# The output gate of the linear attention as one token-major group of 1024 features, and the attention values' writes issued by ScalarE

## The chip, the cores and the metric

The kernel runs on one core of a Trainium2 chip. The metric is the device time of one execution in microseconds (us). Three executions of the kernel before took 965.9, 2431.07 and 965.85 us; the median, 965.9 us, is the figure to beat. A further execution was profiled, and every duration below comes from it.

## The reference, cut to what matters

One layer of a decoder, 512 tokens of 1024 features, fp32, batch 1:

```
h   = RMSNorm(x)
q | k | v | r | low-rank gate | 3 x (attention q, k, v) | gA | gB  =  h @ w_in
oA  = RMSNorm_per_head(gated linear attention(q, k, v)) * silu(r)      4 heads, 256 features each
oB  = dilated attention, 3 groups of 4 heads, group results weighted and added
x  += (sigmoid(gA) * (oA @ w_o_gla) + sigmoid(gB) * (oB @ w_o_attn)) @ w_out
x  += relu(RMSNorm(x) @ w_mlp1)^2 @ w_mlp2
x  += sigmoid(RMSNorm(x) @ w_pg) * (p @ w_pp)
out = RMSNorm(x)
```

The change touches `r`, the gate of the linear attention (1024 columns of w_in), its product with the attention's result oA, and the values v of the attention groups 1 and 2.

## The kernel before, in words

**Products.** An fp32 operand is kept as a pair hi + lo, each of which TensorE takes in one pass; a product is three matmuls, hi·hi, hi·lo and lo·hi. The weights come as 250 operands of 128 x 1024 (512 KB each). `fetch` (L267) walks through them in order: DVE makes lo of operand i (L276), ScalarE hi of operand i+1 (L281), the sums for i+2 are made (`sums`), and the loads for i+3 are issued (`prepare`). Most projections of 512 columns use Winograd's form of Strassen's scheme, with 7 products in place of 8: the operands A11, S1, A22, S2, A12, S4, S3, where S1 = A21 + A22 and S3 = A11 + A21 (up to sign) are sums made by accumulating DMAs that POOL issues into the buffer of the first term (L243 for S1, L258 for S3), and S2 and S4 are sums by DVE (L255, L261). L258 stands right behind L255 in `sums`: DVE's S2 reads A11, then the DMA adds A21 onto A11's buffer, and the seventh product, S3, needs the result.

**Two forms.** `strassen` keeps the weights stationary and streams 256 tokens: 168 matmuls of 256 columns for 512 features, with the result feature-major (a tile holds 128 features). `wide` keeps the activations stationary and streams 512 weight columns: 168 matmuls of 512 columns for 1024 features, with the result token-major (a tile holds 128 tokens x 512 features). In both, ScalarE copies partial sums out of PSUM when a bank has its first product (L369 in `strassen`), and DVE adds the later bank to that copy (`add`, L422).

**Order.** The order on each engine is that of the program text. Every piece of matmuls calls `step`, which takes one callback off the list `later` and lets the first two generators of the list `side` go on by one step per `pace[0]` streamed columns. So work of DVE, ScalarE and POOL, and small groups of matmuls, are laid between the large products by count, not by time. The large products follow each other as k0, q1, k1, q2, k2, v12, v0, gq, gk, gv, oa, r0, r1, gb0, gb1, ga0, ga1, og, wo, then the feed-forward part. v12 (a `wide`), v0, r0 and r1 (each a `strassen`) are those that the change bears on.

**Values.** `values_cls("v12")` makes the values of attention groups 1 and 2. As each of its 8 token-major results is ready, POOL writes it to a DRAM scratch (L767); when a group's fourth is written, POOL reads the four residue classes back by stride (L772). POOL's queue holds, in program order, these writes and reads, the accumulating DMAs L243 and L258, and the exchange of the attention groups' weights: a write of a 16 x 128 tile (L879, `k_dram`) and its read back (L880, `cc`), which DVE's L896 needs.

**Gate.** `gates("r", ...)` runs `strassen` twice (r0, r1). Behind each addition ScalarE applies Sigmoid (L1197) and DVE multiplies (L1201), giving silu(r) as 8 feature-major tiles `rg[j]`. The linear attention runs head by head as generators `gla(h)`: transposes of k by TensorE (L1026), small scores (L1032, L1035), the lo half of the transposed k by DVE (L1039), and products with the values (L976). `gla_out(h)` transposes the head's token-major result (L1126), and DVE multiplies it out of PSUM by the norm's weight and by `rg[j]` (L1129). `gla_split`, started in ga0, makes the pairs `og[j]` (ScalarE L429, DVE L437), which the product og needs.

Of the kernel before, what the change touches and what calls it, by code (L numbers as in the profile page):

```python
# [13 lines left out]
AF = mybir.ActivationFunctionType  # L14
OP = mybir.AluOpType
# [4 lines left out]
P = 128  # L20
T = 512
D = 1024
KC = D // P
# [23 lines left out]
def weight_units():  # L47

    u = []

    def fm(name, src, col, n, row=0):
        for j in range(n):
            u.append((f"{name}.{j}", "fm", src, row, col + j * P))

    def tm(name, src, col):
        for i in range(4):
            u.append((f"{name}.{i}", "tm", src, i * 2 * P, col))

    def quad(name, src, col, kind="quad", chunk=0):
        for m, k in ((0, 0), (1, 0), (1, 1), (0, 1)):  # L60
            u.append((f"{name}.A{m + 1}{k + 1}", kind, src, 2 * chunk + k, col + m * (P if kind == "quad" else 256)))

    def quadw(name, src, cs):

        for m, k in ((0, 0), (1, 0), (1, 1), (0, 1)):
            for i in range(2):
                u.append((f"{name}.A{m + 1}{k + 1}.{i}", "quadw", src, 2 * i + k, cs[m]))

    fm("k0", "w_in", att_col(0, 1), 4)
    fm("q1", "w_in", att_col(1, 0), 4)  # L70
    quad("k1", "w_in", att_col(1, 1))
    quad("q2", "w_in", att_col(2, 0))
    quad("k2", "w_in", att_col(2, 1))
    quadw("v12", "w_in", (att_col(1, 2), att_col(2, 2)))
    quad("v0", "w_in", att_col(0, 2), "quadt")
    quad("gq", "w_in", GQ)
    quad("gk", "w_in", GK)
    quadw("gv", "w_in", (GV, GV + 512))
    for j in range(4):
        u.append((f"oa.{j}", "half", "w_o_attn", 0, j * 2 * P))  # L80
    quad("r0", "w_in", GR)
    quad("r1", "w_in", GR + 512)
    for i in range(2):
        quad(f"gb{i}", "w_in", GATE + D + i * 512)
    for i in range(2):
        quad(f"ga{i}", "w_in", GATE + i * 512)
    fm("og", "w_o_gla", 0, 8)
    fm("wo", "w_out", 0, 8)
    for q in range(8):
        quad(f"m1q{q}", "w_mlp1", q * 512)  # L90
    for what, sub, c in MLP2:
        if what == "plain":
            for kk in range(4 * c, 4 * c + 4):
                u.append((f"m2s{sub}.{kk}", "tm", "w_mlp2", kk * 2 * P, sub * 512))
        else:
            quad(f"m2s{sub}c{c}", "w_mlp2", sub * 512, chunk=c)
    for j in range(2):
        u.append((f"pp{j}.0", "tm", "w_pp", 0, j * 512))
    for j in range(2):
        tm(f"pg{j}", "w_pg", j * 512)  # L100
    return u
# [80 lines left out]
def block_kernel(ctx, tc, xT, ws, pT, wts, wha, wa2, vec, lnf, rel, onehot, ident_d, mask_d, out):  # L182
# [13 lines left out]
    def u32(name="u"):  # L196
        return ar.tile([P, T], F32, tag="u", name=name)
# [11 lines left out]
    side, later = [], []  # L209
# [125 lines left out]
    def halves(t):  # L335
        return slice(t * HT, (t + 1) * HT)
# [47 lines left out]
    def wide(name, xo, finish):  # L384


        bank, sums = {}, {}

        def begin(m, t, n, b):
            def go():  # L390
                sums[m, t, n] = u32()
                S.activation(sums[m, t, n], bank[b][n], AF.Copy, scale=-1.0 if m else 1.0)
            return go

        def end(m, t, n, b):
            return lambda: finish(m, t, n, sums.get((m, t, n)), bank[b][n])

        for i, (op, xname, b) in enumerate(WIDE):
            fresh = b not in bank
            if fresh:  # L400
                bank[b] = [smt() if b == "b" else mmt() for _ in range(2)]
            for pr in range(4):
                wh, wl = weight(f"{name}.{op}.{pr // 2}")
                xh, xl = xo(xname, pr)
                r = slice((pr % 2) * 512, (pr % 2 + 1) * 512)
                mms = []
                for n in range(2):
                    c = slice(n * P, (n + 1) * P)
                    for k, (l, w) in enumerate(((xh, wh), (xl, wh), (xh, wl))):
                        mms.append((bank[b][n], l[:, c], w[:, r], fresh and not pr and not k, pr == 3 and k == 2))  # L410
                run(mms, 3, shared=True)
            if i in WBEGIN:
                (m, t), b = WBEGIN[i]
                later[0:0] = [begin(m, t, n, b) for n in range(2)]
            if i in WEND:
                (m, t), b = WEND[i]
                later.extend(end(m, t, n, b) for n in range(2))
# [8 lines left out]
    def split_hi(x, col=None):  # L426
        hi = u32r()
        if col is None:
            S.activation(hi, x, AF.Copy)  # L429
        else:  # L430
            S.activation(hi, x, AF.Copy, scale=col)
        return hi

    def split_lo(x, hi, col=None):
        lo = u32r()
        if col is None:
            V.tensor_tensor(lo, x, hi.bitcast(F32), op=OP.subtract)  # L437
        else:
            V.scalar_tensor_tensor(out=lo, in0=x, scalar=col, in1=hi.bitcast(F32), op0=OP.mult, op1=OP.subtract)
        return hi, lo  # L440
# [5 lines left out]
    def split_later(x, res, j):  # L446

        def first():
            hi = split_hi(x)
            later.append(lambda: res.__setitem__(j, split_lo(x, hi)))  # L450
        later.append(first)
# [288 lines left out]
    def whole(m, s, ps):  # L740

        if s is None:
            s = u32()
            S.activation(s, ps, AF.Copy, scale=-1.0 if m else 1.0)
        else:
            add(m, s, s, ps)
        return s
# [12 lines left out]
    def values_cls(name):  # L760

        v_dram = [dr.tile([T, 512], F32, name=f"v{m}_dram") for m in range(2)]
        res, left = [[], []], [4, 4]

        def finish(m, t, n, s, ps):
            s, r = whole(m, s, ps), (2 * t + n) * P
            GP.dma_start(v_dram[m][r:r + P, :], s)  # L767
            left[m] -= 1
            if not left[m]:
                for c in range(4):  # L770
                    v = u32()
                    GP.dma_start(v, v_dram[m].rearrange("(m c) f -> c m f", c=4)[c])  # L772
                    res[m].append(v)

        wide(name, xs_op, finish)
        return res

    def softmax(ps, n0, bias, nm, sums, col, prob):
# [338 lines left out]
            yield  # L1117

    def gla_out(h):
        for f in range(2):  # L1120
            j = 2 * h + f
            while rg_done[j] < 2:
                yield
            pts = smt()
            for p in range(4):
                TE.transpose(pts[:, p * P:(p + 1) * P],  # L1126
                             ons_[h][p // 2][:, (p % 2) * 256 + f * P:(p % 2) * 256 + (f + 1) * P], ident)
            yield
            V.scalar_tensor_tensor(out=rg[j], in0=pts, scalar=cv[:, C_GN + j:C_GN + j + 1], in1=rg[j],  # L1129
                                   op0=OP.mult, op1=OP.mult)  # L1130

    def gla_split():
        for j in range(KC):
            split_later(rg[j], og, j)
            yield


    side.append(setup())
# [38 lines left out]
    for j in range(KC):  # L1177
        y = u32()
        S.activation(y, fm(None, oa, (j % 2) * 512, weight(f"oa.{j // 2}")), AF.Copy)
        S.dma_start(y_dram[j], y)  # L1180
    rg, tb, ga = [], [], []
    rg_done = [0] * KC

    def gates(name, i, res, make):

        new = [u32() for _ in range(4)]
        res.extend(new)

        def finish(m, t, s, ps):
            add(m, s, s, ps)  # L1190
            later.append(lambda: make([4 * i + 2 * n + m for n in range(2)], [new[2 * n + m][:, halves(t)] for n in range(2)], s, t))

        strassen(f"{name}{i}", xs_op, finish)

    def silu(js, outs, s, t):
        g = u32()
        S.activation(g, s, AF.Sigmoid)  # L1197

        def mult():
            for n in range(2):  # L1200
                V.tensor_tensor(outs[n], s[:, halves(n)], g[:, halves(n)], op=OP.mult)  # L1201
                rg_done[js[n]] += 1
        later.append(mult)

    def sigmoid(js, outs, s, t):
        for n in range(2):
# [3 lines left out]
        while later:  # L1210
            later.pop(0)()

    gates("r", 0, rg, silu)
    side.extend(gla_out(h) for h in range(2))
    gates("r", 1, rg, silu)
    pace[0] = 4096
    side.extend(gla_out(h) for h in range(2, 4))
    for i in range(2):
        gates("gb", i, tb, sigmoid)

# [9 lines left out]
    later.extend(merge(j) for j in range(KC))  # L1230
    for i in range(2):
        gates("ga", i, ga, sigmoid)
        if i == 0:
            side.append(gla_split())
    drain()
    pace[0] = 2048
    mix = [None] * KC
# [351 lines left out]
    def put(tt, c):  # L1589
        n = c.stop - c.start  # L1590
        o = u32()
        V.scalar_tensor_tensor(out=o[:, 0:n], in0=x2t[4 + tt][:, c], scalar=fr[:, tt:tt + 1], in1=lnb[1][:, c],
                               op0=OP.mult, op1=OP.mult)
        SY.dma_start(out[tt * P:(tt + 1) * P, 512 + c.start:512 + c.stop], o[:, 0:n])
# [112 lines left out]
```

## Time and profile before

| | us |
|---|---|
| median of 3 executions | 965.9 |
| the profiled execution | 968.71 |
| its span, first to last instruction | 966.9 |
| TensorE busy in the span | 954.6 (99%) |
| VectorE (DVE) busy | 740.6 (77%) |
| ScalarE (ACT) busy | 543.9 (56%) |
| POOL busy | 101.5 (10%) |
| mean granted TensorE clock | 0.994 |

PE is TensorE's matmuls, PEld its weight loads, ACTq and POOLq the queues that issue DMAs. In a row of the timeline stand the start, the duration, engine, line, operation, out<-in and, in brackets, how long the engine was idle before and what ended that. In a row of the windows stand the stretch, its length, the busy time of each engine with its number of instructions, the granted clock of TensorE, the share of the DMA engines and GB/s. Groups of instructions have, behind the bar, the total, the mean of one in ns, and the idle time of the engine ahead of them.

### The profile page before, as it was taken

What the parts mean: (1) busy time and instruction counts of PE and PEld (TensorE: products, weight loads), DVE (VectorE), ACT (ScalarE), POOL (GpSimd) and SP (SyncE); (2) the same over time, 40 slices, a digit from 0 to 9 for tenths busy, and PEclk for the clock granted to TensorE, in tenths of its full rate; (3) what the DMA queues carried; (4) which work ended last, traced back from release to release, by engine and by line L of the source; (5) the groups of instructions that cost most, each with busy time, mean ns of one, the idle gap of its engine ahead of it and who ended that gap; (6) DMA issues with size and microseconds to landing.
All of it is one profiled execution on the core that took longest, in us unless ns stands there. A gap on an engine that the chain in (4) does not pass through costs nothing.

```text
span 966.9 us, 16069 instructions
## 1 busy us (share of the span) xinstructions
PE 954.6 (99%) x6398; PEld 880.4 (91%) x6398; DVE 740.6 (77%) x1062; ACT 543.9 (56%) x886; POOL 101.5 (10%) x143
## 2 busy tenths in 40 slices
PE   9999999989999999999999999999999999999997
PEld 8789998889998899999988889999998998998886
DVE  7698879746789669988765788777767999787754
ACT  7357547435575569776632346555655664354633
POOL 0140010220100012023001000010000000000000
PEclk9999999989999999999999999999999999999999
DMA  9374373965636554546526437556564374553102
GB/s 325 116 233 119 117 175 72 300 197 132 147 94 199 170 154 117 146 132 196 153 88 196 131 71 182 162 134 173 155 173 109 110 176 107 134 194 109 44 0 88
DMA packets 42923, 140.97 MB, mean 146 GB/s; under 512 B 6435, under 2 KB 7023, under 8 KB 42848
## 3 DMA queue, kind: packets, MB, share of 16 engines
q1 hardware_dynamic: 28224, 95.37, 29.3%
q0 software_dynamic: 12096, 42.17, 21.5%
q10 hardware_dynamic: 2528, 2.41, 0.7%
q8 instruction: 50, 0.82, 0.3%
q14 instruction: 25, 0.20, 0.1%
HBM read 133.60 MB, written 8.17 MB: 147 GB/s over the span
## 4 chain that ended last, share of the span: by engine, by line
PE 92%; DVE 3%; ACT 2%; DMA 1%; issue 1%; POOL 0%; POOLq 0%; DVEq 0%; ACTq 0%
PE mmt L295 77%; PE smt L295 6%; PE mmt L552 2%; PE smt L976 1%; DMA w<-in_wts_dram 1%; DVE lo L276 1%; PE smt L916 1%; PE smt L839 1%; DVE u L422 0%; PE smt L524 0%; ACT hi L281 0%; PE smt L933 0%; PE smt L809 0%; PE smt L932 0%; PE smt L922 0%
## 5 line engine op out<-in xcount | busy, mean ns | idle before, releaser
L295 PE MATMUL mmt<-ur,hi 128*128 128x256 f32 (+1 forms) x3120 | 635.8, 301 | 0.0
L295 PEld LDWEIGHTS mmt<-ur,hi 128*128 128x128 f32 x3120 | 500.7, 188 | 21.8
L295 PE MATMUL mmt<-ur,lo 128*128 128x256 f32 (+1 forms) x1560 | 470.7, 302 | 0.0
L276 DVE TENSOR_TENSOR lo<-w,hi 128x1024 fp32r<-128x1024 f32 x250 | 303.2, 1219 | 57.3 <-PE mmt L295 27.7
L281 ACT ACTIVATE hi<-w 128x1024 fp32r<-128x1024 f32 x250 | 260.9, 1054 | 110.6 <-PE mmt L295 25.9
L295 PEld LDWEIGHTS mmt<-ur,lo 128*128 128x128 f32 x1560 | 294.0, 188 | 10.9
L295 PE MATMUL mmt<-hi,ur 128*128 128x512 f32 (+3 forms) x480 | 134.7, 366 | 4.3 <-ACT u L369 4.3
L429 ACT ACTIVATE ur<-u 128x512 fp32r<-128x512 f32 x130 | 77.2, 624 | 98.1 <-DVE u L1241 30.8
L295 PEld LDWEIGHTS mmt<-hi,ur 128*128 128x128 f32 x480 | 87.0, 193 | 17.0 <-ACT u L369 4.5
L422 DVE TENSOR_TENSOR u<-u,mmt 128x512 f32<-128x512 f32 (+1 forms) x116 | 73.1, 655 | 38.1 <-PE mmt L295 37.9
L437 DVE TENSOR_TENSOR ur<-u,ur 128x512 fp32r<-128x512 f32 x129 | 84.8, 686 | 16.5 <-ACT ur L429 16.1
L295 PE MATMUL mmt<-lo,ur 128*128 128x512 f32 (+3 forms) x240 | 87.2, 363 | 0.0
L369 ACT ACTIVATE u<-mmt 128x512 f32<-128x512 f32 x88 | 52.3, 594 | 52.8 <-PE mmt L295 52.4
L243 POOL DMA_DIRECT2D w<-in_wts_dram x32 | 28.8, 923 | 309.6 <-DMA w<-in_wts_dram 102.8
L258 POOL DMA_DIRECT2D w<-in_wts_dram x24 | 21.2, 884 | 332.6 <-DVE w L255 239.8
L295 PEld LDWEIGHTS mmt<-lo,ur 128*128 128x128 f32 x240 | 46.3, 193 | 6.6
L295 PE MATMUL smt<-ur,hi 128*128 128x512 f32 x160 | 50.4, 393 | 0.1
L295 PEld LDWEIGHTS smt<-ur,hi 128*128 128x128 f32 x160 | 29.7, 188 | 8.1 <-PE smt L649 0.8
L295 PE MATMUL smt<-ur,lo 128*128 128x512 f32 x80 | 31.2, 390 | 0.0
L255 DVE TENSOR_TENSOR w<-w 128x1024 f32<-128x1024 f32 x24 | 29.4, 1225 | 0.8
L261 DVE TENSOR_TENSOR w<-w 128x1024 f32<-128x1024 f32 x24 | 29.4, 1225 | 0.8
L462 ACT ACTIVATE u<-u 128x512 f32<-128x512 f32 x24 | 14.9, 622 | 16.7 <-DVE u L1322 16.7
(213 smaller groups left out, 767.8 us busy)
## 6 DMA issues: line engine op xcount, KB each, us to landing
w<-in_wts_dram SPq DMA_DIRECT2D x170, 512.0 KB, 4.4
w<-in_wts_dram POOLq DMA_DIRECT2D x56, 512.0 KB, 5.7
u<-in_xT_dram SPq DMA_DIRECT2D x8, 256.0 KB, 5.0
u<-in_ws_dram SPq DMA_DIRECT2D x8, 256.0 KB, 5.2
v_dram<-u POOLq DMA_DIRECT2D x8, 256.0 KB, 9.1
u<-v_dram POOLq DMA_DIRECT2D x8, 256.0 KB, 6.1
y_dram<-u ACTq DMA_DIRECT2D x8, 256.0 KB, 3.6
u<-y_dram POOLq DMA_DIRECT2D x8, 256.0 KB, 5.9
```

The source lines that it names most:

```text
L243: GP.dma_start(w, wts[UNIT[b]], accum_op=OP.add)
L255: V.tensor_tensor(w, w, raw[f"{q}.A11"], op=OP.add)
L258: GP.dma_start(w, wts[UNIT[f"{q}.A21"]], accum_op=OP.add)
L261: V.tensor_tensor(w, w, raw[f"{q}.A12"], op=OP.add)
L276: V.tensor_tensor(lo, w, hi.bitcast(F32), op=OP.subtract)
L281: S.activation(hi, w, AF.Copy)
L295: TE.matmul(o, lhsT=l, rhs=r, start=a, stop=b, skip_group_check=shared)
L369: S.activation(sums[c], bank[b], AF.Copy, scale=-scale if c[0] else scale)
L422: V.tensor_tensor(out, s, ps, op=OP.subtract if m else OP.add)
L429: S.activation(hi, x, AF.Copy)
L437: V.tensor_tensor(lo, x, hi.bitcast(F32), op=OP.subtract)
L552: TE.matmul(q0ps[i], lhsT=(hi, hi, lo)[j][:, c], rhs=(xh, xl, xh)[j], start=not k and not j, stop=k == KC - 1 and j == 2)
```

## The change

It has three parts.

1. The two `strassen` of the gate, r0 and r1, become one `wide("r")` on 1024 columns. Sigmoid and product are one ScalarE and one DVE instruction of 128 x 512 per result, and silu(r) is kept as 8 token-major tiles `rg[m, 2t + n]`.
2. `gla_out(h)` waits for the four gate tiles of its half, multiplies the head's token-major result by them in place (four DVE instructions of 128 x 256), then transposes, and the pair `og[j]` is made straight out of PSUM, the norm's weight as the scale. `gla_split` is gone. All four `gla_out` are put on the side list ahead of the gate's product, and the line that set the pace to 4096 from r1 on is gone, so it stays 3072 through gb0 to ga1.
3. In `values_cls` the 8 writes go onto ScalarE's queue, each as a callback behind the addition, and the 8 reads are issued by a generator that starts when all 8 writes are issued.

```diff
-    quad("r0", "w_in", GR)
-    quad("r1", "w_in", GR + 512)
+    quadw("r", "w_in", (GR, GR + 512))
...
         def finish(m, t, n, s, ps):
             s, r = whole(m, s, ps), (2 * t + n) * P
-            GP.dma_start(v_dram[m][r:r + P, :], s)
-            left[m] -= 1
-            if not left[m]:
+
+            def put():
+                S.dma_start(v_dram[m][r:r + P, :], s)
+                left[0] -= 1
+            later.append(put)
+
+        def back():
+            while left[0]:
+                yield
+            yield
+            for m in range(2):
                 for c in range(4):
                     v = u32()
                     GP.dma_start(v, v_dram[m].rearrange("(m c) f -> c m f", c=4)[c])
                     res[m].append(v)
+                yield
 
         wide(name, xs_op, finish)
+        side.append(back())
...
     def gla_out(h):
+        while not all((h // 2, p) in rg for p in range(4)):
+            yield
+        for p in range(4):
+            o = ons_[h][p // 2][:, halves(p % 2)]
+            V.tensor_tensor(o, o, rg[h // 2, p][:, halves(h % 2)], op=OP.mult)
+            if p % 2:
+                yield
         for f in range(2):
             j = 2 * h + f
-            while rg_done[j] < 2:
-                yield
             pts = smt()
...
             yield
-            V.scalar_tensor_tensor(out=rg[j], in0=pts, scalar=cv[:, C_GN + j:C_GN + j + 1], in1=rg[j],
-                                   op0=OP.mult, op1=OP.mult)
-
-    def gla_split():
-        for j in range(KC):
-            split_later(rg[j], og, j)
-            yield
+            c = cv[:, C_GN + j:C_GN + j + 1]
+            hi = split_hi(pts, c)
+            yield
+            og[j] = split_lo(pts, hi, c)
...
-    def silu(js, outs, s, t):
-        g = u32()
-        S.activation(g, s, AF.Sigmoid)
-
-        def mult():
-            for n in range(2):
-                V.tensor_tensor(outs[n], s[:, halves(n)], g[:, halves(n)], op=OP.mult)
-                rg_done[js[n]] += 1
-        later.append(mult)
+    def silu(m, t, n, s, ps):
+        s, g = whole(m, s, ps), u32()
+
+        def act():
+            S.activation(g, s, AF.Sigmoid)
+
+            def mult():
+                V.tensor_tensor(s, s, g, op=OP.mult)
+                rg[m, 2 * t + n] = s
+            later.append(mult)
+        later.append(act)
...
-    gates("r", 0, rg, silu)
-    side.extend(gla_out(h) for h in range(2))
-    gates("r", 1, rg, silu)
-    pace[0] = 4096
-    side.extend(gla_out(h) for h in range(2, 4))
+    side.extend(gla_out(h) for h in range(4))
+    wide("r", xs_op, silu)
...
         gates("ga", i, ga, sigmoid)
-        if i == 0:
-            side.append(gla_split())
```

POOL's queue around the end of v12 and through v0, before. L243 is an accumulation for S1, L258 for S3, L767 and L772 the writes and reads of the values, L879 and L880 the weights' exchange; the L258 in the middle is that of v0.

```order
L243 DMA w<-in_wts_dram 128x1024 x5
L767 DMA v_dram<-u 128x512 x4
L243 DMA w<-in_wts_dram 128x1024
L767 DMA v_dram<-u 128x512 x2
L772 DMA u<-v_dram 128x512 x4
L258 DMA w<-in_wts_dram 128x1024
L767 DMA v_dram<-u 128x512 x2
L772 DMA u<-v_dram 128x512 x4
L879 DMA k_dram<-u 16x128
L880 DMA cc<-k_dram 128x4x4
```

The same place in the changed kernel, where L243 is L242, L258 is L257, L772 is L779, and L879 and L880 are L888 and L889.

```order
L257 DMA w<-in_wts_dram 128x1024 x2
L242 DMA w<-in_wts_dram 128x1024 x6
L257 DMA w<-in_wts_dram 128x1024
L779 DMA u<-v_dram 128x512 x8
L888 DMA k_dram<-u 16x128
L889 DMA cc<-k_dram 128x4x4
```

The writes have left POOL's queue, v0's L257 stands ahead of all eight reads instead of behind the first four, and k_dram and cc still stand behind the last read.

ScalarE's queue at the same place in the changed kernel: L280 makes hi (L281 before), L768 are the writes, L743 and L368 copies out of PSUM.

```order
L280 ACTIVATE hi<-w 128x1024 x2
L768 DMA v_dram<-u 128x512 x2
L280 ACTIVATE hi<-w 128x1024 x2
L743 ACTIVATE u<-mmt 128x512 x2
L870 ACTIVATE e_1988<-e_1988 128x16
L871 ACTIVATE e_1989<-e_1989 128x16
L768 DMA v_dram<-u 128x512
L280 ACTIVATE hi<-w 128x1024
L368 ACTIVATE u<-mmt 128x512
L768 DMA v_dram<-u 128x512
L280 ACTIVATE hi<-w 128x1024
```

The rows shown are the last of three pairs of writes and the last two single ones; the seventh and eighth write stand at the start of v0's products, between hi operands.

TensorE around the linear attention's third head (h = 2), before: L1026 are its transposes of k (the second L1026 those of the fourth head), L976 its first products with the values, L295 the large products (here those of r1 and gb0).

```order
L1026 MATMUL smt<-ident,u 128x128 x3
...
L1032 MATMUL smt<-u 128x64 x4
L1035 MATMUL smt<-u 64x64 x4
...
L1026 MATMUL smt<-ident,u 128x128 x3
...
L295 MATMUL mmt<-ur,hi 128x256 x2
L976 MATMUL smt<-ur 128x256 x6
```

The same in the changed kernel (L1026 is L1035, L1032 and L1035 are L1041 and L1044, L976 is L985, L295 is L294; the large products are the end of `wide("r")` and then gb0).

```order
L1035 MATMUL smt<-ident,u 128x128 x3
L294 MATMUL mmt<-hi,ur 128x512 x2
...
L1041 MATMUL smt<-u 128x64 x4
L1044 MATMUL smt<-u 64x64 x4
...
L294 MATMUL mmt<-ur,hi 128x256
L985 MATMUL smt<-ur 128x256 x6
```

Before, 88 matmuls of 256 columns lie between the head's transposes and its first products with the values; after, 18 of 512 columns and 40 of 256, and the fourth head's transposes come later.

More of the change, by code (lines that the diff above doesn't have):

```diff
@@ L762, in values_cls @@
         v_dram = [dr.tile([T, 512], F32, name=f"v{m}_dram") for m in range(2)]
-        res, left = [[], []], [4, 4]
+        res, left = [[], []], [8]
         def finish(m, t, n, s, ps):
             s, r = whole(m, s, ps), (2 * t + n) * P
-            GP.dma_start(v_dram[m][r:r + P, :], s)
-            left[m] -= 1
-            if not left[m]:
+            def put():
[7 more added lines that the diff above has]
+            for m in range(2):
                 for c in range(4):
@@ L1180, in block_kernel @@
         S.dma_start(y_dram[j], y)
-    rg, tb, ga = [], [], []
-    rg_done = [0] * KC
+    rg, tb, ga = {}, [], []
     def gates(name, i, res, make):
```

## Prediction

> **What bounds the kernel now.** I read the profile's page first, then TensorE's waits, then the chain of waits, the timeline and the windows around the one long wait. The page:
>
> ```profile
> span 966.9 us, 16069 instructions
> PE 954.6 (99%) x6398; PEld 880.4 (91%) x6398; DVE 740.6 (77%) x1062; ACT 543.9 (56%) x886; POOL 101.5 (10%) x143
> ```
>
> TensorE is busy for 954.6 of 966.9 us. A gain can only be shorter matmul work or less of the 12 us of idling. Where TensorE waits for another engine:
>
> ```profile
> PE mmt L295 <- ACT u L369: 4.3, 1, 4.3
> PE smt L524 <- POOL ones L519: 1.0, 1, 1.0
> PE smt L976 <- DVE ur L1039: 0.2, 1, 0.2
> PE smt L916 <- ACT u L908: 0.2, 1, 0.2
> ```
>
> Columns: total us, times, longest. One wait of 4.3 us stands out. The chain of waits around it (start, us, what) and the timelines of POOL, DVE and TensorE:
>
> ```profile
> 194.34 0.44 POOL u L772
> ...
> 194.86 11.38 DMA w<-in_wts_dram
> ...
> 206.32 0.07 ACT hi L281
> ...
> 209.35 2.71 PE mmt L295 x11
> ```
>
> ```profile
> 192.75 2.13 POOL L772 DMA_DIRECT2D u<-v_dram  x4 [8.77 <-DMA v_dram<-u]
> 194.86 0.94 POOL L258 DMA_DIRECT2D w<-in_wts_dram  x1
> 195.42 1.48 POOL L767 DMA_DIRECT2D v_dram<-u  x2
> 208.43 2.14 POOL L772 DMA_DIRECT2D u<-v_dram  x4 [11.53 <-issue]
> 216.75 0.79 POOL L880 DMA_DIRECT2D cc<-k_dram  x1 [5.68 <-DMA k_dram<-u]
> ```
>
> ```profile
> 184.30 1.23 DVE L255 TENSOR_TENSOR w<-w 128x1024 f32<-128x1024 f32 x1
> ```
>
> ```profile
> 209.35 0.79 PE L295 MATMUL mmt<-hi,ur 128*128 128x256 f32 x2 [4.26 <-ACT u L369]
> ```
>
> The profile names ScalarE's copy L369, but the chain shows who was late. TensorE waits at v0's seventh product for hi of S3, which ScalarE starts only at 206.32, when the accumulation L258 has landed (11.38 us after its issue at 194.86). DVE's sum, behind which that DMA may go, ended at 185.53. It was issued 9.3 us later because POOL's queue had the first four value reads ahead of it, and POOL stood 8.77 us waiting for the value writes to land. Then the granted clock:
>
> ```profile
> core 0: us, PE busy (x) PEld busy (x) DVE busy (x) ACT busy (x) POOL busy (x), PEclk, DMA share, GB/s
> 187.60:204.80 17.20, 17.20 (x146) 17.14 (x145) 5.87 (x11) 4.11 (x8) 4.16 (x7) 1.00 0.78 240
> 204.80:209.40 4.60, 0.34 (x4) 0.13 (x2) 1.78 (x2) 3.08 (x5) 0.97 (x2) 0.91 0.13 46
> 209.40:215.30 5.90, 5.90 (x28) 5.90 (x29) 4.65 (x6) 3.44 (x4) 1.67 (x4) 0.50 0.82 265
> ```
>
> After the idle, 28 matmuls take 5.90 us at a clock of 0.50. The 146 of the first stretch took 17.20 us, 0.118 each, so 28 need 3.30. The clock costs 5.90 − 3.30 = 2.6 us, and the wait with its tail 4.26 + 2.6 = 6.9 us. The Trainium skill, "TensorE: Matmul & The Clock Gate", Part 1, has the clock drop to 4/8 after an idle window of about 3.4 µs and come back after a busy one; the row of 0.50 agrees, though the slow stretch here is longer than one such window.
>
> **The change part by part.**
>
> *Values' writes (part 3).* With the writes gone from POOL's queue and the reads behind L257, v0's accumulation goes when DVE's sum ends, at about 186. How long it takes to land:
>
> ```profile
> w<-in_wts_dram POOLq DMA_DIRECT2D x56, 512.0 KB, 5.7
> v_dram<-u POOLq DMA_DIRECT2D x8, 256.0 KB, 9.1
> ```
>
> Median 5.7 us, here 11.38: issued at 186.1 it lands at 192 to 197.5. From hi's start at 206.32 to TensorE's at 209.35 are 3.0 us, and TensorE is out of work at 209.35 − 4.26 = 205.1, so hi has to start by 202.1. Even at the longer landing 4.6 us are left. So the wait goes, and with it the half clock: **−6.9 us**. The bounds are 0 (a landing later by 4.6 us and the whole wait more) and −6.9, since TensorE has no other idle time there.
>
> What ScalarE takes over is 8 issues. POOL's own take
>
> ```profile
> L767 POOL DMA_DIRECT2D v_dram<-u x8 | 4.8, 648 | 4.9 <-DVE u L422 4.7
> 160.00:180.00 20.00, 20.00 (x90) 16.25 (x89) 16.16 (x19) 12.32 (x21) 3.08 (x5) 1.00 0.61 170
> 180.00:200.00 20.00, 20.00 (x139) 18.66 (x138) 12.10 (x20) 7.69 (x11) 6.17 (x10) 1.00 0.82 276
> ```
>
> 0.65 us each, 5.2 us in all, with up to 4.7 us of waiting for DVE's additions; ScalarE is idle for 20 of these 40 us. Behind a waiting issue stand hi operands, which are made an operand ahead; one of v12's 14 operands lasts TensorE 12 matmuls of 0.226 us (below), 2.7 us, so a write that waits a microsecond delays no product. I cost it at nothing; without this cover it would be at most the 5.2 us.
>
> What is late next: the reads of both groups. They wait for the last write, which stands behind v0's first copy on ScalarE, and DVE's consumer of cc stands behind k_dram and cc:
>
> ```profile
> 190.76 0.60 ACT L369 ACTIVATE u<-mmt 128x512 f32<-128x512 f32 x1 [1.31 <-PE mmt L295]
> 221.22 0.62 DVE L896 TENSOR_SCALAR u<-u,cc 128x256 f32<-128x256 f32 x2 [1.91 <-DMA cc<-k_dram]
> ```
>
> The last write goes at 191.4 instead of 196.9 and lands by 200.5 (9.1 later); the eight reads then take 2 x 2.13 us to issue, to 204.8, where before the last was issued at 210.6. k_dram needs 0.5 + 5.7 us (the wait in front of L880), cc about as much: it lands by 216.5 at the latest. It is needed 6.9 us earlier than before, at 212.4 to 214.3. So DVE waits 0 to 4 us where it waited 1.91, and TensorE went on meanwhile. I cost it at nothing; its upper bound is 2 us.
>
> *Gate as one wide group (part 1).* 336 matmuls of 256 columns become 168 of 512. Two stretches with almost only the one kind:
>
> ```profile
> 620.00:720.00 100.00, 100.00 (x845) 100.00 (x844) 73.62 (x85) 57.99 (x83) 7.72 (x9) 1.00 0.61 159
> 500.00:560.00 60.00, 60.00 (x266) 49.70 (x265) 38.11 (x56) 21.28 (x29) 6.12 (x10) 1.00 0.50 150
> ```
>
> 100 / 845 = 118.3 ns for 256 columns, with weight loads busy for all of it; 60 / 266 = 225.6 ns for 512, with the loads 83% busy. Thus 336 x 0.1183 = 39.75 against 168 x 0.2256 = 37.9: **−1.8 us**. Missing records would make both a little shorter: with 0.6 ns to either side the bounds are −1.5 and −2.1. The Trainium skill, "TensorE: Matmul & The Clock Gate", section "Back-to-back issue gap", gives N / 2.4 + 2.5 ns for a warm matmul, an estimate of 109 and 216 ns, by which 36.7 − 36.2 = −0.5 us; the rows are 9 and 10 ns above it and decide.
>
> The other engines' share:
>
> ```profile
> L422 DVE TENSOR_TENSOR u<-u,mmt 128x512 f32<-128x512 f32 x92 | 61.2, 684 | 33.1 <-PE mmt L295 32.9
> L437 DVE TENSOR_TENSOR ur<-u,ur 128x512 fp32r<-128x512 f32 x129 | 84.8, 686 | 16.5 <-ACT ur L429 16.1
> L1201 DVE TENSOR_TENSOR u<-u 128x256 f32<-128x256 f32 x16 | 6.0, 421 | 0.6 <-ACT u L1197 0.6
> L1129 DVE SCALAR_TENSOR_TENSOR u<-smt,cv,u 128x512 f32<-128x512 f32 x8 | 6.0, 745 | 0.0
> ```
>
> DVE: two additions fewer (two results have a single bank), −1.4; 16 products of 421 ns become 8 of about 684, −1.2; 16 new products of the token-major result at 421, +6.7; eight L1129 and eight L437 become eight lo straight from PSUM at 745, −5.5. Sum −1.4 us, so DVE's total hardly moves. ScalarE's hi now reads PSUM, its copies stay 8; SP loads A11's two operands a second time, as S3 overwrites them. The transposes of L1126 stay 32. None of this sets the end.
>
> *What moves in time.* The gate's stretch is where DVE and ScalarE have least room:
>
> ```profile
> 340.70:366.99 26.29, 26.29 (x226) 26.16 (x225) 17.40 (x27) 20.43 (x36) 2.26 (x3) 1.00 0.50 134
> 366.99:388.70 21.71, 21.71 (x185) 21.71 (x184) 19.43 (x36) 21.11 (x40) 5.72 (x5) 1.00 0.58 147
> 388.70:414.51 25.81, 25.60 (x221) 25.13 (x219) 24.48 (x42) 17.39 (x31) 2.25 (x3) 1.00 0.49 123
> ```
>
> These are r0, r1 and gb0. In gb0 DVE is busy for 24.48 of 25.81 us, and TensorE's only other wait falls there:
>
> ```profile
> 387.41 0.49 PE L1026 MATMUL smt<-ident,u 128*128 128x128 f32 x3
> ...
> 400.80 0.74 PE L976 MATMUL smt<-ur 128*128 128x256 f32 x4 [0.21 <-DVE ur L1039]
> ```
>
> Head 2's transposed k left TensorE at 387.41, its first products with the values were due 12.8 us later (400.19 or so, two of them went), and DVE's lo came 0.21 us late. Of these, 88 x 0.118 = 10.4 us were large matmuls and 2.4 transposes of two heads and scores. In the changed kernel 18 matmuls of 512 and 40 of 256 columns stand there, 18 x 0.226 + 40 x 0.118 = 8.8 us, and some 2.1 for one head's transposes and the scores: 10.9 us. So 1.9 us less, and DVE is the engine that is due: lo may be late by 1.9 + 0.2 = 2.1. Against that, the earlier half of the gate's work has room (17.40 of 26.29), and the order lists two table loads of ScalarE fewer, 1.28 us each:
>
> ```profile
> 390.13 1.28 ACT L1197 ACT_TABLE_LOAD   x1
> ```
>
> The bounds are 0 and +2.1; the slack of 2.3 us that DVE had in r1 (21.71 − 19.43) makes the lower one the nearer, so I take **+0.8 us**. An idle time of up to 2.1 us is shorter than the one that dropped the clock.
>
> **Sum.** −6.9 − 1.8 + 0.8 = −7.9 us. On the profiled execution: 968.71 − 7.9 = 960.8. That execution is 2.8 us above the median of 965.9, and the terms are the same on either, so 965.9 − 7.9 = **958.0 us**, −0.8%.
>
> **Rivals.**
>
> *The accumulation lands late all the same.* For it: the DMA engines are 78% busy over v0 and the landing took 11.38 us, twice the median. The writes now come sooner and more densely, ahead of it on the same engines. Against it: 4.6 us of room. If it keeps the wait, the change gives −1.8 + 0.8: **964.9 us**. The Trainium skill, "DMA: Bandwidth & Descriptors", section "Issuing engines are not separate DMA queues", says that issuing on several engines only saves the sequencer's time to issue; by that rule this is the result. The 8.77 us are POOL's waiting in queue order, not issue time, and no bandwidth is needed for them to go. 8 in 100.
>
> *DVE late at several heads.* Room in gb0 is 1.3 us, and the pace no longer goes to 4096, so the steps of heads 2 and 3 come a third closer together. If lo of k or of the gate's operands is late at three or four places by 1 to 1.5 us, 3 to 5 us go: 965.9 − 8.7 + 3 to 5 = **960 to 962**. Against it: −1.4 us of DVE work in all. 17 in 100.
>
> *Slower than before: one long wait in the gate's stretch with the half clock.* The wait for lo of head 2 grows past the 4.3 us that dropped the clock at 209. It then costs itself and 2.6 us. To outweigh −8.7 it has to be over 6.1 us: DVE's room of 2.3 and 1.3 us would have to turn into 6 us of arrears. At 7 us of wait: 965.9 − 8.7 + 9.6 = **966.8 us**. For it: DVE at 95% of gb0. Against it: DVE has 1.4 us less to do, and the tightening is 1.9 us. 4 in 100.
>
> *The stall goes, but matmuls of 512 do not gain here.* In r the small matmuls of the heads break the stream as well; then −6.9 + 0.8 and **959.8**. It lies within the likeliest case's range.
>
> **How the numbers follow.** The likeliest (71 in 100) is 958.0, its own range 956.5 to 960: from −1.8 − 6.9 with nothing late, 957.2, and with the matmul bound of −2.1, 956.9, to +2.1 late, 959.3. The rivals above reach 962 and 964.9. The range is **956 to 963**: the lower end allows 0.9 us for what I have not seen, the upper one takes in the second rival; out of it lie the first and the third rival with 12 in 100. A measurement of this kernel can tell about 2% (19.3 us) from no change. No case reaches that on the fast side, and on the slow side only something unforeseen: faster 0.01, same 0.97, slower 0.02.
>
> **What would show it right or wrong.** In the profile after, v0's L257 is issued before 188 and no PE wait of over 1 us stands in v0; the clock is 1.00 from 188 to 220. From the gate's first product to gb0's first are 46 us in place of 48.0. TensorE's waits name L1048 (lo of k) with 0 to 2.1 us. If v0's wait is still there, the queue was not its cause; if TensorE has a wait of over 3 us between 330 and 420, the second or third rival holds; if gb0's start is less than 1 us nearer to the gate's, the matmul term is wrong.

## The result, and the profile after

The changed kernel took 960.33 us (median of 6 executions, 959.87 to 960.66), the kernel before, on the same chip, 967.38 us; the ratio is 0.9928, 95% interval 0.9914 to 0.9943. One execution of the kernel before (2431.07 us) and one of the last kernel below (1576.4 us, granted clock 0.556) were slow by far and are left out of the ratios and ranges; without them the medians are 967.3 and 962.9 us. In three later jobs, on which the experiments rest, the kernel before had medians of 965.57, 965.09 and 964.47 us with single executions from 962.3 to 968.5, the changed kernel 959.91 us. So the level of the changed kernel is firm, and what scatters is the kernel before: in the last of these jobs the two stood 4.56 us apart, not 7.05.

The page of the changed kernel and TensorE's waits:

```profile
span 958.5 us, 15733 instructions
PE 950.3 (99%) x6230; PEld 869.3 (91%) x6230; DVE 739.4 (77%) x1060; ACT 542.0 (57%) x884; POOL 95.3 (10%) x135
```

```profile
PE smt L523 <- POOL ones L518: 1.0, 1, 1.0
PE smt L1140 <- DVE u L1133: 0.2, 1, 0.2
```

The wait of 4.3 us is gone, and of the waits inside the kernel one of 0.2 us is left, at a new place: the transposes L1140 wait for DVE's products with the gate, L1133. POOL's timeline, and the first hi behind the accumulation on ScalarE:

```profile
185.82 0.87 POOL L257 DMA_DIRECT2D w<-in_wts_dram  x1 [3.54 <-DVE w L254]
193.91 2.19 POOL L779 DMA_DIRECT2D u<-v_dram  x4 [7.22 <-PE mmt L294]
198.00 2.12 POOL L779 DMA_DIRECT2D u<-v_dram  x4 [1.90 <-issue]
208.13 0.80 POOL L889 DMA_DIRECT2D cc<-k_dram  x1 [7.50 <-DMA k_dram<-u]
```

```profile
195.66 1.06 ACT L280 ACTIVATE hi<-w 128x1024 fp32r<-128x1024 f32 x1 [1.67 <-DMA w<-in_wts_dram]
```

v0's accumulation goes when DVE's sum ends, 9 us earlier than before, and hi of S3 is made 10.7 us earlier. The reads still wait for the writes' landing, but nothing that TensorE needs soon stands behind them. The windows of v0's end, and of the gate's stretch as a whole (r to ga1), first after, then before:

```profile
204.80:209.40 4.60, 4.60 (x41) 4.60 (x41) 2.59 (x5) 2.12 (x2) 0.99 (x2) 1.00 0.10 35
209.40:215.30 5.90, 5.90 (x51) 5.71 (x50) 5.87 (x15) 1.67 (x4) 1.61 (x2) 1.00 0.78 158
...
333.04:474.45 141.41, 141.25 (x1041) 133.38 (x1039) 119.75 (x180) 104.60 (x199) 21.90 (x27) 1.00 0.58 156
```

```profile
340.70:483.22 142.52, 142.31 (x1209) 141.70 (x1208) 118.24 (x177) 106.51 (x201) 23.97 (x27) 1.00 0.55 151
```

No idle time and no half clock are left in v0. By stage, from each product's first matmul to the next one's, v0 went from 26.95 to 20.14 us, gq from 32.03 to 31.44 (the rest of the half clock and a wait of 0.2), and the gate's stretch from 142.52 to 141.41. That is −6.8, −0.6 and −1.1; with −0.25 at the start and about +0.4 behind ga1 the span fell by 8.4 us.

### The profile page after: what moved, and what is told of

The parts are those of the page before. It is cut to its first block, busy times and chain, and to the rows that moved or that the text cites. A ratio compares the mean times of both kernels' runs of the same rounds, so it can differ in the third digit from the quotient of the medians.

```text
span 958.5 us, 15733 instructions
## 1 busy us (share of the span) xinstructions
PE 950.3 (99%) x6230; PEld 869.3 (91%) x6230; DVE 739.4 (77%) x1060; ACT 542.0 (57%) x884; POOL 95.3 (10%) x135
## 4 chain that ended last, share of the span: by engine, by line
PE 96%; DVE 1%; issue 1%; ACT 1%; DMA 1%; POOL 0%; POOLq 0%; DVEq 0%; ACTq 0%
PE mmt L294 80%; PE smt L294 7%; PE mmt L551 2%; PE smt L985 1%; PE smt L925 1%; PE smt L848 1%; DMA u<-y_dram 1%; PE smt L523 0%; PE smt L818 0%; PE smt L942 0%; PE smt L941 0%; PE smt L931 0%; PE smt L817 0%; PE smt L1547 0%; PE smt L1041 0%
## 5 line engine op out<-in xcount | busy, mean ns | idle before, releaser
L294 PE MATMUL mmt<-ur,hi 128*128 128x256 f32 (+1 forms) x2896 | 594.8, 303 | 0.0
L294 PEld LDWEIGHTS mmt<-ur,hi 128*128 128x128 f32 x2896 | 465.9, 188 | 21.8
L294 PE MATMUL mmt<-ur,lo 128*128 128x256 f32 (+1 forms) x1448 | 438.9, 303 | 0.0
L280 ACT ACTIVATE hi<-w 128x1024 fp32r<-128x1024 f32 x250 | 261.1, 1054 | 105.3 <-PE mmt L294 30.0
L294 PEld LDWEIGHTS mmt<-ur,lo 128*128 128x128 f32 x1448 | 272.7, 188 | 10.9
L294 PE MATMUL mmt<-hi,ur 128*128 128x512 f32 (+3 forms) x576 | 162.5, 367 | 0.0
L428 ACT ACTIVATE ur<-u 128x512 fp32r<-128x512 f32 x122 | 72.3, 624 | 96.8 <-DVE u L1248 30.9
L294 PEld LDWEIGHTS mmt<-hi,ur 128*128 128x128 f32 x576 | 102.5, 188 | 15.9
L294 PE MATMUL mmt<-lo,ur 128*128 128x512 f32 (+3 forms) x288 | 105.0, 365 | 0.0
L436 DVE TENSOR_TENSOR ur<-u,ur 128x512 fp32r<-128x512 f32 x121 | 79.5, 685 | 16.6 <-ACT ur L428 16.2
L368 ACT ACTIVATE u<-mmt 128x512 f32<-128x512 f32 x80 | 47.4, 593 | 47.6 <-PE mmt L294 47.3
L242 POOL DMA_DIRECT2D w<-in_wts_dram x34 | 31.3, 959 | 335.1 <-DMA w<-in_wts_dram 139.0
L294 PEld LDWEIGHTS mmt<-lo,ur 128*128 128x128 f32 x288 | 54.2, 188 | 8.6
L257 POOL DMA_DIRECT2D w<-in_wts_dram x22 | 19.6, 889 | 319.2 <-DVE w L254 231.1
L294 PE MATMUL smt<-ur,hi 128*128 128x512 f32 x160 | 50.4, 393 | 0.1
L294 PEld LDWEIGHTS smt<-ur,hi 128*128 128x128 f32 x160 | 29.7, 188 | 8.1 <-PE smt L648 0.8
L294 PE MATMUL smt<-ur,lo 128*128 128x512 f32 x80 | 31.2, 390 | 0.0
```

What stands on the lines that cost most here:

```text
L242: GP.dma_start(w, wts[UNIT[b]], accum_op=OP.add)
L257: GP.dma_start(w, wts[UNIT[f"{q}.A21"]], accum_op=OP.add)
L280: S.activation(hi, w, AF.Copy)
L294: TE.matmul(o, lhsT=l, rhs=r, start=a, stop=b, skip_group_check=shared)
L368: S.activation(sums[c], bank[b], AF.Copy, scale=-scale if c[0] else scale)
```

## The experiments

**Part 3 alone.** The kernel before with the change's `values_cls` and nothing else of it.

> The kernel before with part 3 alone: the eight value writes on ScalarE's queue, the reads issued by the generator after the last write. The gate stays as before. My theory (POOL's queue order made v0's accumulation late; the half clock follows from the wait) expects v0 to take 20.1 us instead of 26.95, gq 31.4 instead of 32.0, no TensorE wait of over 1 us and the clock at 1.00 throughout: 7.4 us less in the trace, a ratio of 0.9924 (0.991 to 0.994). The rival, that most of the gain comes from the gate, expects 0.997 or more.

960.90 against 965.57 us, ratio 0.9949 (0.9931 to 0.9967). In its trace v0 takes 20.14 us and gq 31.42, and no wait of TensorE is over 1.0 us. So the trace behaves as forecast, but the gain between executions is 4.7 us and not 7.4, and the ratio lies outside the 0.991 to 0.994 that I expected. Part 3 is most of the change; my size for it is too large.

**Parts 1 and 2 alone.** The changed kernel with the old `values_cls`.

> The changed kernel with the values' writes and reads as before (POOL, in the old order), so parts 1 and 2 alone. My theory expects the wait of 4.3 us and the half clock in v0 to stand as before, and 1.1 us less over the gate's stretch (r to ga1, 142.5 us before): a ratio of 0.9989 (0.998 to 1.000). The rival, that the gate's change gains more than its matmuls show, expects below 0.997.

964.41 us, ratio 0.9991 (0.9977 to 1.0004). The stretch r to ga1 takes 141.63 us. TensorE's wait in v0 is there, smaller than in the first profile, and the clock falls all the same (its timeline, then two windows with the granted clock, third from the end):

```profile
207.21 0.51 PE L294 MATMUL mmt<-hi,ur 128*128 128x256 f32 x2 [2.42 <-ACT u L368]
```

```profile
204.51:207.92 3.41, 0.99 (x9) 0.78 (x8) 2.44 (x3) 3.41 (x5) 0.69 (x2) 1.00 0.26 43
207.92:211.33 3.41, 3.41 (x19) 3.41 (x18) 3.38 (x5) 1.43 (x3) 1.94 (x4) 0.50 0.83 309
```

**Writes left on POOL, only the reads moved.**

```diff
         def finish(m, t, n, s, ps):
             s, r = whole(m, s, ps), (2 * t + n) * P
             GP.dma_start(v_dram[m][r:r + P, :], s)
-            left[m] -= 1
-            if not left[m]:
-                for c in range(4):
-                    ...
+            left[0] -= 1
+
+        def back():
+            ...
         wide(name, xs_op, finish)
+        side.append(back())
```

> The kernel before, with the eight writes left on POOL's queue and only the reads moved behind the last write (the generator). v0's accumulation then stands behind six writes but ahead of all reads. My theory (the reads' wait for the writes' landing is what held the queue) expects the same as with part 3 alone: no wait in v0, ratio 0.9924 (0.991 to 0.994). The rival, that the writes need ScalarE's queue, expects the wait to stay above 2 us and a ratio above 0.996.

960.55 us, ratio 0.9948 (0.9932 to 0.9964): the whole gain of part 3 (as there, short of the 0.991 to 0.994 expected), with no instruction moved to ScalarE. POOL's timeline:

```profile
182.56 1.22 POOL L767 DMA_DIRECT2D v_dram<-u  x2 [0.60 <-DVE u L422]
185.91 0.90 POOL L258 DMA_DIRECT2D w<-in_wts_dram  x1 [2.12 <-DVE w L255]
187.91 1.22 POOL L767 DMA_DIRECT2D v_dram<-u  x2 [1.11 <-ACT u L744]
191.72 2.13 POOL L777 DMA_DIRECT2D u<-v_dram  x4 [2.59 <-DMA v_dram<-u]
```

The accumulation stands behind six writes and is on time, since a write waits only for DVE's addition. What held it was the reads.

**Writes on ScalarE, the reads where they were.** The kernel before, with the write as a callback on ScalarE's queue and, in the same callback, each group's four reads on POOL behind its fourth write.

```diff
-            GP.dma_start(v_dram[m][r:r + P, :], s)
-            left[m] -= 1
-            if not left[m]:
-                for c in range(4):
-                    ...
+            def put():
+                S.dma_start(v_dram[m][r:r + P, :], s)
+                left[m] -= 1
+                if not left[m]:
+                    for c in range(4):
+                        ...
+            later.append(put)
```

> The kernel before, with the writes on ScalarE's queue but each group's reads on POOL as soon as its four writes are issued, so four reads stand ahead of v0's accumulation as before. My theory expects POOL to wait for the writes' landing again, the accumulation to go after 192, and the wait in v0 to be 2 to 5 us: ratio 0.994 to 1.000. The rival, that the issuing engine makes the difference, expects no wait in v0 and 0.9924.

964.44 us, ratio 0.9993 (0.9980 to 1.0007): no gain. The timelines of POOL, ScalarE and TensorE, then two windows that share the wait:

```profile
191.03 2.18 POOL L774 DMA_DIRECT2D u<-v_dram  x4 [9.32 <-DMA v_dram<-u]
193.18 0.96 POOL L258 DMA_DIRECT2D w<-in_wts_dram  x1
...
203.50 1.06 ACT L281 ACTIVATE hi<-w 128x1024 fp32r<-128x1024 f32 x1 [10.09 <-DMA w<-in_wts_dram]
...
206.52 0.39 PE L295 MATMUL mmt<-hi,ur 128*128 128x256 f32 x1 [2.36 <-ACT u L369]
```

```profile
201.99:205.41 3.42, 2.17 (x19) 1.96 (x17) 0.82 (x1) 1.92 (x3) 0.00 (x0) 1.00 0.90 349
205.41:208.82 3.41, 2.30 (x19) 2.30 (x20) 3.21 (x4) 2.95 (x4) 1.34 (x2) 1.00 0.55 167
```

POOL waits 9.32 us for the landing of writes that ScalarE issued, and the accumulation behind it goes at 193.18. The Trainium skill, "DMA: Bandwidth & Descriptors", section "Issuing engines are not separate DMA queues", says that another issuing engine saves no more than the time to issue; this kernel agrees. TensorE's wait of 2.36 us leaves the clock at 1.00, where one of 2.42 in the kernel with parts 1 and 2 dropped it.

The traces show in what the two waits differ. In every trace of this case the changes of the granted clock lie whole steps of 3.41 us apart; in the first profile it fell at 208.54 and came back two steps later, at 215.37. In the kernel with parts 1 and 2 the whole wait lay inside one step, 204.51 to 207.92, in which TensorE worked for only 0.99 us, and the next step ran at 0.50. Here a step ends at 205.41, in the middle of the wait, and leaves 1.25 us of idling in one step and 1.11 in the next. So the place of the wait goes with the fall, and not only its length; how much idling in a step it takes is not shown.

**The accumulation made late, with nothing ahead of it.** The changed kernel with 10, and with 15, small operations of POOL in front of v0's accumulation.

```diff
+            if q == "v0":
+                for _ in range(10):
+                    GP.tensor_tensor(idle, idle, mh, op=OP.pow)
             GP.dma_start(w, wts[UNIT[f"{q}.A21"]], accum_op=OP.add)
```

> The changed kernel with ten small POOL operations (a power of a 128 x 4 scratch tile, about 0.7 us each, nothing reads it) put ahead of v0's accumulation, which so goes at about 191.5 instead of 185.8, with no value write or read ahead of it. My theory (only the accumulation's landing counts) expects it to land by 197 to 202, and no wait or one under 1 us: a time within 1 us of the changed kernel, ratio 0.993 to 0.996, with a small spread. The rival, that the writes and reads themselves disturb TensorE or ScalarE in v0, expects the same, so this run alone does not tell them apart; the next one does.

> The same with fifteen operations: v0's accumulation goes at about 195, as in the kernel before (194.86), still with no write or read ahead of it. My theory expects the wait in v0 back: 2 to 5 us, with a half clock behind it in some executions and in others not, so a spread of 2 us or more between executions and a ratio of 0.995 to 1.001. The rival, that the reads' traffic made the wait, expects none and 0.993 to 0.995.

The operations took 1.3 us each and not 0.7, so the issues came at 194.86 and 200.51. The first is, to the hundredth, the time of the kernel before. The timelines with ten (961.65 us, ratio 0.9965, 0.9954 to 0.9977):

```profile
181.62 13.28 POOL L259 TENSOR_TENSOR idle<-idle,mh 128x4 f32<-128x4 f32 x10
194.86 0.92 POOL L260 DMA_DIRECT2D w<-in_wts_dram  x1
...
202.41 1.06 ACT L283 ACTIVATE hi<-w 128x1024 fp32r<-128x1024 f32 x1 [9.07 <-DMA w<-in_wts_dram]
...
205.44 0.50 PE L297 MATMUL mmt<-hi,ur 128*128 128x256 f32 x2 [1.20 <-ACT u L371]
...
212.63 0.57 PE L930 MATMUL smt<-ident,u 128*128 128x128 f32 x3 [1.23 <-DVE u L910]
```

Hi starts 7.6 us after the issue, against 11.5 us in the kernel before, where four reads of 256 KB were issued right ahead. The wait is 1.20 us instead of 4.26, and a second one of 1.23 us follows in gq, for DVE, which has worked with hardly a break since S3's operand landed. That is a little more than I expected (a wait under 1 us, a ratio of at most 0.996). So it is not the issue alone that counts: the time to landing differs too, presumably with what else is under way. That the four reads make the 4 us is not shown, for in the changed kernel, with no read ahead of it, the accumulation took 9.8 us. With fifteen (966.96 us, ratio 1.0018, 1.0007 to 1.0028, where I expected at most 1.001) the wait is back in full, without any read or write ahead, as its timelines and a window show:

```profile
200.51 0.92 POOL L260 DMA_DIRECT2D w<-in_wts_dram  x1
...
209.34 0.79 PE L297 MATMUL mmt<-hi,ur 128*128 128x256 f32 x2 [4.86 <-ACT u L371]
```

```profile
210.00:214.00 4.00, 4.00 (x26) 4.00 (x26) 3.77 (x6) 2.01 (x3) 0.80 (x1) 0.70 0.71 281
```

A late landing alone, here through a late issue, makes the wait and, behind it, the lower clock. The executions spread over 2.6 us (965.37 to 967.93).

**The changed kernel with its writes on POOL.** The edit of `finish` above, in the changed kernel.

> The changed kernel with the eight value writes back on POOL's queue, the reads behind the last write as in the change. My theory expects the same time as the changed kernel (ratio 0.994 to 0.995 against before, within 0.5 us of it), since in the kernel with part 3 alone ScalarE's queue was not needed. The rival, that ScalarE's queue helps once the gate is wide, expects 1 us more.

959.83 us, ratio 0.9949 (0.9934 to 0.9964), within 0.5 us of the changed kernel's 959.91 to 960.33. ScalarE's queue adds nothing with the wide gate either.

**One more step between products and transposes.** In the changed kernel's `gla_out`:

```diff
             if p % 2:
                 yield
+        yield
         for f in range(2):
```

> The changed kernel with one more step between DVE's products and the transposes in the gated output of each head. My theory (the transposes L1140 of the second head wait 0.6 us for DVE's products L1133) expects that wait gone, the 32 transposes at 2.84 us as before instead of 3.59, and 0.6 us less over the gate's stretch (141.4 us); that is 0.06% of the time, which the comparison cannot show. The rival, that the transposes are slower for another reason (their operand was just written), expects 3.5 us for them still.

959.44 us, ratio 0.9944 (0.9930 to 0.9957). L1140 (L1141 here) no longer waits, and its 32 transposes take 2.84 us from start to start.

**Four kernels without the wait, on one chip.** Part 3 alone, the change, the change with the step, and the change with one line more behind the gate's product:

```diff
     wide("r", xs_op, silu)
+    pace[0] = 4096
```

> The kernel with part 3 alone once more, now on the same chip as the next three, none of which has the wait in v0. The four differ by the gate's stretch only, so their medians can be set against each other. My theory expects this one 1.1 us above the changed kernel (1.5 us of large matmuls gained by it, 0.75 us lost at the transposes, 0.4 us gained at L976). The rival, that the wide gate gains nothing on TensorE, expects the two equal within 0.3 us.

> The changed kernel itself, beside the other three. My theory: 1.1 us under the kernel with part 3 alone, 0.7 us above the one with a step between. The rival expects the same as part 3 alone.

> The changed kernel with one more step between DVE's products and the transposes, beside the other three. My theory: 0.7 us under the changed kernel, as the transposes' row fell from 3.59 to 2.84 us. The rival, that the step only moves the wait, expects no difference within 0.3 us.

> The changed kernel with the pace at 4096 again from gb0 on, as it was before from r1 on. If DVE is the tight engine in the gate's stretch because the steps come closer together (the prediction's second rival), the wait at L1140 goes and 0.3 to 1 us are gained. My theory, that this wait is a matter of one step's distance, expects the later steps to push the last heads' transposes towards og, and a time within 0.5 us of the changed kernel.

| kernel | us, median (lowest to highest) | r to ga1 in the trace | ratio to before, 95% |
|---|---|---|---|
| part 3 alone | 960.28 (960.20 to 960.38) | 142.49 | 0.9951 (0.9935 to 0.9967) |
| the change | 959.91 (959.53 to 961.02) | 141.47 | 0.9949 (0.9934 to 0.9964) |
| the change, one step between | 959.06 (958.87 to 959.56) | 140.61 | 0.9939 (0.9924 to 0.9953) |
| the change, pace 4096 | 962.9 (962.12 to 963.83) | 144.93 | 0.9983 (0.9973 to 0.9994) |

The stretch follows my theory of the first three to 0.2 us. The medians show 0.37 us of the 1.0 between the first two, since the stretch is not all that differs between two executions (their starts differ by some tenths, and part 3 alone spreads less), and 0.85 us for the step. The kernel with the step is the fastest of the four, though its range just touches that of the changed kernel. The last kernel refutes the rival and, in the time, my own theory: a larger pace does push the transposes towards og, but it makes the wait at L1140 longer, not shorter, and costs 3.0 us. Its waits of TensorE and its timeline:

```profile
PE smt L1140 <- DVE u L1133: 2.9, 2, 1.7
```

```profile
438.57 0.66 PE L1140 MATMUL smt<-ident,u 128*128 128x128 f32 x2 [1.20 <-DVE u L1133]
...
473.73 0.82 PE L1140 MATMUL smt<-ident,u 128*128 128x128 f32 x6
476.26 1.10 PE L1140 MATMUL smt<-ident,u 128*128 128x128 f32 x6 [1.72 <-DVE u L1133]
```

At 4096 the steps of the last head do not fit into ga1 any more. What is left is drained at its end with no large products between, and twelve transposes stand there in a row, waiting for the products that DVE has just been given. That the line fell away is thus a part of the change by itself, worth 3 us in the changed kernel.

## Why the prediction was right or wrong

**That the wait in v0 goes, and why.** Right. The accumulation went at 185.8, and hi of S3 at 195.66 had 6 us of room where I gave 4.6. The wait is queue order: moving the reads alone brings the gain, moving the writes alone does not. I had credited the writes' move and the reads' move together; the writes' is idle.

**−6.9 us for it.** The trace pair gives −7.4, the executions −4.7 (ratio 0.9949, so 3.2 to 6.7 us). The step that failed is the sentence that the terms are the same on the profiled execution and on the median. The profiled one, 968.71 us, had a long wait with the half clock; later executions go down to 962.3, and the two other traces that keep the early reads show waits of 2.42 and 2.36 us, one with the clock's fall and one without. Over v0 and gq they take 4.2 and 3.6 us more than the trace of part 3 alone (55.74 and 55.19 against 51.56), the profiled one 7.4. 965.9 − 4.7 − 1.1 = 960.1, which is near the 960.33 measured, so nearly all of the 2.3 us between 958.0 and 960.33 lies in this term. The wait on this landing is not one length, and the 2.8 us by which the profiled execution stood above the median were a sign of it, which I noted and did not use. That the ratio of the result, 0.9928, comes so near to the forecast of 0.992 is luck in part: the kernel before stood at 967.3 there, and against its 964.47 in the last job the same change gives 0.9949.

**−1.8 us for the matmuls.** −1.5 in the trace. From start to start, over the gate's stretch:

```
                         before                     after
256 columns, large       1007 x 119.8 ns = 120.67   672 x 120.1 ns = 80.71
512 columns, large                                  167 x 230.2 ns = 38.44
products with values     111 -> 13.70               111 -> 13.25
transposes of the output  32 ->  2.84                32 ->  3.59
other small              54 ->  5.10                54 ->  5.10
```

The 512-column price was taken from og and wo, which nothing interrupts; v12, a `wide` with small matmuls between, runs at 230.6 ns in the trace of before, and that row was nearer. This is the last rival's mechanism, at a sixth of the term. (The estimate beside the term, −0.5, should read −0.4, 36.3 against 36.7; nothing rests on it.)

**+0.8 us for lo of k.** Right to its length, wrong in its end. Between head 2's transposes and its products with the values now lie 10.86 us (375.08 to 385.94), where I had worked out 10.9. But DVE is not late:

```profile
384.40 0.55 DVE L1048 TENSOR_TENSOR ur<-smt,ur 128x384 fp32r<-128x384 f32 x1
...
385.94 0.88 PE L985 MATMUL smt<-ur 128*128 128x256 f32 x6
```

It ends at 384.95, 1 us ahead, and the products with the values even take 0.45 us less in all. In its place 0.75 us went to a place that I had passed over, the transposes behind the new in-place products:

```profile
436.84 0.38 PE L1140 MATMUL smt<-ident,u 128*128 128x128 f32 x2
437.38 0.66 PE L1140 MATMUL smt<-ident,u 128*128 128x128 f32 x2 [0.16 <-DVE u L1133]
```

The change made a wait that had no counterpart (DVE ahead of the transposes, where before it came only behind them), and I had priced its work, not its place in the order. The step between took the wait away, so it is shown. The gate's sum, −1.0 forecast and −1.1 measured, is right by luck: its misses cancel.

**What else was said to be seen.** From the gate's first product to gb0's are 48.16 us and not 46: small matmuls of the heads moved forward out of gb into r, so that stretch alone was the wrong one to look at; r to ga1 shows the gain. Cc landed at about 210.5 (2.4 us after its issue), and DVE no longer waits for it.

**The rivals.** A late landing in spite of the order did not happen, but its ground was half right: the landing took 9.8 us and not the median of 5.7, and over these traces it came between 5.8 and 11.4 us after the issue. The rival of a pace that makes DVE late had the sign wrong. No long wait arose in the gate's stretch; the kernel with the larger pace comes nearest to it, and there it is 1.72 us.

What stays open: how often the kernel before has the longer wait, since only three traces of kernels with the early reads show its length. On the clock's part the mean granted clock of each execution, which is on record, says something: of the 61 executions of the kernel before in the three later jobs, the 16 at 0.994 or 0.995 have a median of 966.98 us, the 45 at 0.996 or more 964.53, with a range of 962.34 to 968.5. So the lower clock goes with some 2.5 us, and a good part of the scatter is there without it.

## What to carry to other kernels

A DMA that waits for data holds every DMA behind it on its engine's queue (here 8.8 and 9.3 us on POOL's); put the ones that somebody waits for ahead of those that themselves wait, and only then ask which engine issues them. A wait at a transfer's landing is not one number: compare the profiled execution with the spread of the others before its length is taken as the gain. Where a product is moved ahead of a transposition, look whether TensorE now waits for it; here a step between the two took away 0.8 us.

## What the runs showed of the hardware

- The clock fell after 2.42 us of TensorE idling in one kernel, to 0.50 for 3.41 us, and not after 2.36 us in another. Its changes lie whole steps of 3.41 us apart in every trace; the first wait lay inside one step, the second across two. The Trainium skill, "TensorE: Matmul & The Clock Gate", Part 1, gives a window of about 3.4 µs that runs freely; that the fall hangs on more than the idle's length agrees, but an idle time below the window is no protection, though I had assumed so.
- The same accumulating DMA of 512 KB had its result used 5.8, 7.6, 9.8 and 11.5 us after issue, in the kernels with fifteen and with ten operations ahead, the changed kernel and the kernel before. What else was under way differed between them; the share of each transfer is not shown.
- A power of a 128 x 4 tile on POOL took 1.3 us.
